# A hybrid encoder trunk on one core: where the up product's weight sums are made, and a seven-product down multiplication for the first token block

## The chip, the cores and the metric

The kernel runs on one core of one Trainium2 chip. The metric is the device time of one execution in microseconds. A core has TensorE (PE, matrix products, with its weight load shown apart as PEld), VectorE (DVE), ScalarE (ACT), GpSimd (POOL) and SyncE (SP), which here issues every DMA.

## What is computed

One layer of the trunk for 2048 prompt tokens and 32 sample tokens (2080 in all), model width 1024. A mixer (spatial gating and a gated delta rule) comes first; what the change alters is the feed-forward part behind it and its weights:

```python
    m, nb, ns, vr = mixer(h, conv_state[l], delta_state[l], w_in[l], ...)
    x = x + gt1 * m
    h = rmsnorm(x, norm_ffn_g[l]) * (1 + sc2) + sh2
    x = x + gt2 * (jnp.square(jax.nn.relu(h @ w_up[l])) @ w_down[l])
...
y = rmsnorm(x, final_norm_g)
```

`w_up` is 1024 x 4096 and `w_down` is 4096 x 1024, all float32.

## The kernel before

**Precision.** A float32 value is split into a high part, rounded to fp32r by ACT, and a low part, the difference, made by DVE (`split`, line 824; `operand`, line 1425). A product is three matmuls: high by high, high by low, low by high (`mm3`, line 411).

**Order of the work.** The whole program is written down as operations with an engine, a cost and the memory they touch (`Program.op`, line 218). `schedule` (line 237) then plays them through a model of the engines and puts them into one order. Where several are ready on an engine, a priority decides (`CHAIN, INV, LOCAL, EVAC, GEMM, IDLE`, line 55); from EVAC on, the place of the matmul that needs the result. On the chip each engine, SP too, runs its part of that order strictly from front to back, and waits where an operand or a buffer isn't there.

**The mixers** (`mixers`, line 856) take the first part of the time: input projections with weight slabs, the delta rule per head (`delta_local`, `delta_inv`, `delta_chain`), gating, and the output projection (`out_stage`, line 1331). `consts` (line 689) stands at their start. In `delta_chain` (line 1233) a chunk of 128 tokens goes PE, DVE, PE, ACT, PE, DVE, and the state `S` that the DVE writes last is what the next chunk's PE work reads.

**The feed-forward** (`feed_forward`, line 1509) goes over four token blocks of 520 tokens (two halves of 260). Per block there are 16 slabs of the hidden width (256 channels each). `ffn_up` (line 1572) multiplies a slab as 2x2 blocks by seven block products instead of eight (the Strassen-Winograd scheme): the token side's sums were made earlier (`h2_values`), the weight side needs four sums of the four weight blocks a11, a12, a21, a22. Two slabs form one step q of the down product. `ffn_down` (line 1674) does it by seven block products per half u of a step, `ffn_down8` (line 1715) by eight. Which one is taken is decided by `plain` (line 1506): for all steps of block 0, and for the last step of every block, the eight.

**Sums of the weights.** `up_weights(b, s)` (line 1430): in block 0 the four blocks are loaded, POOL makes the four sums (128x512 each), all seven operands are split (ACT and DVE), and the high and low parts of the four sums are written to memory (`su_d`, eight tiles of 128x512 a slab). Blocks 1 to 3 load three plain blocks, which are split, and the eight stored parts, which ACT alone rounds. `down_weights` (line 1469): block 0 loads and splits four plain blocks, and for even u makes the four sums on POOL and stores them (`sd_d`); in block 1 the sums of odd u are made the same way (`down_sums`, line 1484); otherwise they are loaded.

**Hidden values.** `hidden` (line 1626) splits the squared relu values into operands. With eight products there are four operands a slab; with seven there are seven for two slabs and each half-channel m, and four of them need a subtraction of 128x260, on POOL. Rings of buffers: `uraw` six buffers and `draw` four in block 0, joined to one ring of eight behind slab 15 of block 0; `rp8` for the hidden operands of block 0, `rpa` and `rpb` in the others.

Of the kernel before, what the change touches and what calls it, by code (L numbers as in the profile page):

```python
# [9 lines left out]
F32R = mybir.dt.float32r  # L10
AF = mybir.ActivationFunctionType
ALU = mybir.AluOpType
# [4 lines left out]
P = 128  # L17
# [101 lines left out]
class View:  # L119
# [55 lines left out]
    def pbc(self, n):  # L175
        return self.step("partition_broadcast", np.broadcast_to(np.uint8(0), (n,) + self.shape), self.reg, n)

# [145 lines left out]
class Kern:  # L323
# [211 lines left out]
    def setup(self):  # L535
# [74 lines left out]
        rg("va", [(q, 256 * e) for q in (18, 19, 20) for e in range(4)][:10], (P, 256))  # L610
        rg("raw", hv(18), (P, 516))
# [24 lines left out]
        self.su_d = [[[dt(f"su_d{s}_{i}{e}", [P, 512]) for e in range(2)] for i in range(4)] for s in range(16)]  # L636
# [52 lines left out]
    def consts(self):  # L689
# [3 lines left out]
        with self.p.at(GEMM):  # L693
# [19 lines left out]
            self.fill(self.z0, 0.0)  # L713

# [715 lines left out]
    def up_weights(self, b, s):  # L1430

        quad = lambda q: self.i["w_u"][s, q]
        if b == 0:
            a11, a12, a21, a22 = (self.raw(self.uraw, quad(q)) for q in range(4))
            s1, s2 = (self.turn(self.uraw) for _ in range(2))
            self.tt(s1, a21, a22, ALU.add, POOL)
            self.tt(s2, s1, a11, ALU.subtract, POOL)
        out = []

        def sum_(i, x):  # L1440
            if b == 0:
                hl = self.operand(self.uw, x)
                for e in range(2):
                    self.dma(self.su_d[s][i][e], hl[e].f32())
            else:
                hl = self.turn(self.uw)
                for e in range(2):
                    self.act(hl[e], self.raw(self.uraw, self.su_d[s][i][e]), AF.Copy)
            out.append(hl)

        plain = lambda q, x: out.append(self.operand(self.uw, x if b == 0 else self.raw(self.uraw, quad(q))))
        if b:
            s1 = s2 = s3 = s4 = a11 = a12 = a22 = None
        plain(0, a11)
        sum_(1, s2)
        sum_(0, s1)
        if b == 0:
            s3 = self.turn(self.uraw) if len(self.uraw) > 6 else a11
            self.tt(s3, a11, a21, ALU.subtract, POOL)
        sum_(2, s3)  # L1460
        if b == 0:
            s4 = s2
            self.tt(s4, a12, s2, ALU.subtract, POOL)
        sum_(3, s4)
        plain(1, a12)
        plain(3, a22)
        return out

# [377 lines left out]
```

## Time and profile before

| | us |
|---|---|
| runs shown: median (lowest to highest of 3) | 2415.27 (2406.06 to 2415.52) |
| the profiled execution's own time | 2432.54 |
| its span, first to last instruction | 2430.8 |
| mean granted TensorE clock | 0.996 |
| busy: PE, PEld, DVE, ACT, POOL | 2363.7, 2209.3, 1728.4, 1551.2, 757.9 |

The profiled execution is 17.3 us above the median of the runs. The stages in the trace: mixers from 0 to 1047 us, then the four token blocks, whose borders are at 1403, 1746 and 2084 us, and the end at 2431. Rows of groups read: line, engine, operation, written<-read tiles, shape, count, then busy time, mean ns of one, and the idle time before them with what ended it. Tile names: `f` is a PSUM bank of the feed-forward, `g`, `C`, `L`, `B`, `M` are PSUM banks of the mixers, `wh` and `wl` slab buffers for high and low parts, `BH` and `BL` the activations' high and low parts, `s` any of 25 SBUF slots, `wr` a raw weight buffer.

### The profile page before, as it was taken

The page shows a single profiled execution, that of the slowest core. Times are in us where ns is not written, and L with a number is a line of the kernel's source. Part 1 is how long each engine was busy: PE and PEld are TensorE (multiplying, and loading weights), DVE is VectorE, ACT ScalarE, POOL GpSimd, SP SyncE. Part 2 cuts the span into 40 slices and gives each one's busy share as a digit, 9 for nine tenths or more (in the row PEclk, how much of TensorE's full clock was granted, in tenths as well). Part 3 has the DMA queues.
Part 4 walks back from the last instruction along what each step waited for, and adds up shares of the span by engine and source line. Part 5 has one row for each costly group of instructions (what it writes and reads, how often), then busy time and mean ns, then how long its engine had stood idle before and what let it go on. Part 6 is the DMA issues. An engine that isn't in the chain of part 4 may idle for free.

```text
span 2430.8 us, 53532 instructions
## 1 busy us (share of the span) xinstructions
PE 2363.7 (97%) x18834; PEld 2209.3 (91%) x18834; DVE 1728.4 (71%) x3993; ACT 1551.2 (64%) x3705; POOL 757.9 (31%) x1055
## 2 busy tenths in 40 slices
PE   7999999999999999999999999999999999999998
PEld 4877778999989878999999999999999999999998
DVE  5556666556664646477777778889788878878796
ACT  4555556465655435365554688777897877877774
POOL 2134523212433223444434353323431212511111
PEclk9999999999999999999999999999999999999999
DMA  8688668455557767888766778786888878876773
GB/s 302 212 280 301 199 192 262 136 180 163 149 167 218 240 189 240 267 266 257 274 217 218 256 245 275 235 292 231 271 284 275 273 237 263 256 251 224 244 232 111
DMA packets 387238, 570.38 MB, mean 235 GB/s; under 512 B 71356, under 2 KB 201296, under 8 KB 386968
## 3 DMA queue, kind: packets, MB, share of 16 engines
q1 hardware_dynamic: 386968, 566.96, 72.5%
q8 instruction: 148, 2.42, 0.4%
q14 instruction: 122, 1.00, 0.1%
HBM read 432.44 MB, written 134.35 MB: 233 GB/s over the span
## 4 chain that ended last, share of the span: by engine, by line
PE 55%; DMA 17%; ACT 9%; DVE 9%; issue 5%; POOL 3%; SPq 1%; DVEq 0%; POOLq 0%; ACTq 0%
PE f L398 25%; PE g L398 22%; DVE s L352 5%; ACT s L337 5%; DMA s<-su_d 4%; PE C L398 3%; POOL s L352 2%; DMA s<-w_u 2%; ACT wh L337 2%; PE B L398 2%; DVE wl L352 1%; DVE s L357 1%; PE L L398 1%; SPq L390 1%; ACT wl L337 1%
## 5 line engine op out<-in xcount | busy, mean ns | idle before, releaser
L337 ACT ACTIVATE s<-s 128x260 fp32r<-128x260 f32 (+9 forms) x1379 | 601.6, 463 | 300.4 <-DVE s L357 82.0
L398 PE MATMUL f<-s,s 128*128 128x260 f32 x4068 | 541.3, 283 | 6.5 <-DVE s L352 4.9
L352 POOL TENSOR_TENSOR s<-s,s 128x260 f32<-128x260 f32 (+3 forms) x354 | 358.5, 1024 | 532.7 <-ACT s L337 400.1
L398 PE MATMUL f<-BH,wh 128*128 128x260 f32 x1796 | 511.1, 285 | 12.7 <-DVE s L352 11.1
L398 PEld LDWEIGHTS f<-s,s 128*128 128x128 f32 x4068 | 508.7, 188 | 11.0 <-DVE s L352 7.2
L398 PE MATMUL f<-BH,wl 128*128 128x260 f32 x1796 | 507.7, 283 | 1.1 <-DVE wl L352 1.1
L398 PE MATMUL f<-BL,wh 128*128 128x260 f32 x1796 | 506.4, 282 | 0.1
L352 DVE TENSOR_TENSOR s<-s,s 128x512 fp32r<-128x512 f32 (+5 forms) x721 | 412.3, 586 | 97.6 <-ACT s L337 63.4
L398 PE MATMUL g<-BH,wh 128*128 128x512 f32 (+2 forms) x1112 | 422.2, 380 | 0.0
L352 DVE TENSOR_TENSOR s<-f,s 128x260 f32<-128x260 f32 x856 | 345.0, 420 | 97.9 <-PE f L398 90.3
L398 PE MATMUL g<-BH,wl 128*128 128x512 f32 (+2 forms) x1112 | 392.9, 353 | 0.0
L398 PE MATMUL g<-BL,wh 128*128 128x512 f32 (+2 forms) x1112 | 391.6, 352 | 0.6 <-DVE BL L352 0.6
L398 PEld LDWEIGHTS f<-BH,wh 128*128 128x128 f32 x1796 | 337.7, 188 | 16.7 <-DVE s L352 8.2
L398 PEld LDWEIGHTS f<-BH,wl 128*128 128x128 f32 x1796 | 338.2, 188 | 1.9 <-DVE wl L352 1.9
L398 PEld LDWEIGHTS f<-BL,wh 128*128 128x128 f32 x1796 | 338.5, 188 | 0.3 <-DVE BL L352 0.3
L352 POOL TENSOR_TENSOR s<-s 128x260 f32<-128x260 f32 (+11 forms) x315 | 155.2, 493 | 475.7 <-DVE s L352 239.5
L337 ACT ACTIVATE wh<-s 128x512 fp32r<-128x512 f32 (+1 forms) x369 | 230.3, 630 | 78.6 <-DMA s<-w_u 28.3
L398 PEld LDWEIGHTS g<-BH,wh 128*128 128x128 f32 x1112 | 211.1, 190 | 26.6 <-issue 9.5
L398 PEld LDWEIGHTS g<-BH,wl 128*128 128x128 f32 x1112 | 210.2, 189 | 19.4
L398 PE MATMUL f<-BH,s 128*128 128x260 f32 x1016 | 225.5, 284 | 0.9 <-DVE s L352 0.8
L398 PEld LDWEIGHTS g<-BL,wh 128*128 128x128 f32 x1112 | 211.1, 190 | 15.0 <-DVE BL L352 1.1
L357 DVE SCALAR_TENSOR_TENSOR s<-s,s,s 128x512 f32<-128x512 f32 (+6 forms) x318 | 164.2, 533 | 76.0 <-ACT s L337 38.4
(119 smaller groups left out, 3537.7 us busy)
## 6 DMA issues: line engine op xcount, KB each, us to landing
s<-su_d SPq DMA_DIRECT2D x288, 256.0 KB, 3.9
s<-w_u SPq DMA_DIRECT2D x171, 256.0 KB, 4.2
s<-w_d SPq DMA_DIRECT2D x151, 256.0 KB, 4.2
s<-sd_d SPq DMA_DIRECT2D x106, 256.0 KB, 4.1
wr<-su_d SPq DMA_DIRECT2D x96, 256.0 KB, 4.4
wr<-w_b SPq DMA_DIRECT2D x42, 512.0 KB, 4.7
wr<-w_d SPq DMA_DIRECT2D x70, 256.0 KB, 4.8
s<-x_d SPq DMA_DIRECT2D x128, 130.0 KB, 3.9
```

The lines of the kernel that those rows point to most:

```text
L337: self.p.op(ACT, c, lambda: nc.scalar.activation(out=R(out), in_=R(in_), func=func, **{k: R(v) for k, v in kw.items()}), [out, accum], [in ...
L352: self.p.op(eng, c, lambda: e.tensor_tensor(out=R(out), in0=R(a), in1=R(b), op=op), [out], [a, b])
L357: self.p.op(DVE, c, lambda: nc.vector.scalar_tensor_tensor(out=R(out), in0=R(a), scalar=R(s), in1=R(b), op0=op0, op1=op1), [out], [a, s, b])
L390: self.p.op(DMA, max(500, x), lambda: nc.sync.dma_start(out=R(out), in_=R(in_)), [out], [in_], lat=DMA_LATENCY + min(0, x - 500))
L398: nc.tensor.matmul(R(out), R(l), R(r), **kw)
```

## The change

1. A method `up_sums` is called at the end of `consts`, with the lowest priority `IDLE`. It goes over the 16 slabs in four pieces of 128 columns each (64 pieces). A piece loads all four blocks by one DMA (128x4x128), makes the four sums in place on DVE (128x128 each), stores the four sums, and then twice rounds half of them on ACT (128x256) and stores the remainder that DVE forms (128x256). The first store holds the unrounded sums, the other two the low parts: the "two parts" in memory.
2. `up_weights` does in block 0 what blocks 1 to 3 did: three plain blocks loaded and split, eight stored parts loaded and rounded by ACT. POOL's sums and the eight stores a slab are gone from block 0.
3. `plain` is true for step 7 alone: block 0 does steps 0 to 6 by seven products. Its down sums are made in block 0 for all u below 14 (POOL, stored), and block 1 loads all of them.
4. The subtractions of the hidden values run on DVE in block 0, and on POOL in the others as before.
5. The rings are joined from the start, and `rp8` is gone.

```diff
@@ setup
+        rg("sh", [(8, 512), (9, 0), (10, 768), (14, 784)], (P, 2, 128))
+        rg("sx", [(4, 0), (4, 512)], (P, 4, 128))
...
-        self.su_d = [[[dt(f"su_d{s}_{i}{e}", [P, 512]) for e in range(2)] for i in range(4)] for s in range(16)]
+        self.su_d = [[dt(f"su_d{s}_{e}", [P, 4, 512]) for e in range(2)] for s in range(16)]
@@ consts
+        with self.p.at(IDLE):
+            self.up_sums()
+
+    def up_sums(self):
+
+        for n in range(64):
+            s, c = n // 4, slice(128 * (n % 4), 128 * (n % 4) + 128)
+            x = self.new("sx")
+            self.dma(x, self.i["w_u"][s, :, :, c].rearrange("q p c -> p q c"))
+            a11, a12, a21, a22 = (x[:, q] for q in range(4))
+            self.tt(a22, a21, a22, ALU.add)
+            self.tt(a21, a11, a21, ALU.subtract)
+            self.tt(a11, a22, a11, ALU.subtract)
+            self.tt(a12, a12, a11, ALU.subtract)
+            self.dma(self.su_d[s][0][:, :, c], x)
+            for h in (slice(2, 4), slice(0, 2)):
+                y = self.new("sh")
+                self.cp(y.f32r(), x[:, h], ACT)
+                self.tt(y, x[:, h], y, ALU.subtract)
+                self.dma(self.su_d[s][1][:, h, c], y)
@@ up_weights
+        for i, q in ((None, 0), (0, None), (3, None), (2, None), (1, None), (None, 1), (None, 3)):
+            if i is None:
+                out.append(self.operand(self.uw, self.raw(self.uraw, self.i["w_u"][s, q])))
+                continue
+            hl = self.turn(self.uw)
+            for e in range(2):
+                self.act(hl[e], self.raw(self.uraw, self.su_d[s][e][:, i]), AF.Copy)
             out.append(hl)
@@ down_sums
-        if b == 1 and u % 2:
+        if b == 0:
             a11, a12, a21, a22 = (get(quad(q)) for q in range(4))
-            s1, s2 = (self.turn(self.draw) for _ in range(2))
+            s1 = self.turn(self.draw)
...
-    def plain(self, b, q):
-        return b == 0 or q == 7
+    def plain(self, q):
+        return q == 7
@@ hidden
+        eng = POOL if b else DVE
         if s % 2 == 0 and g == 0:
             put("B11", t)
-            self.tt(k0, k1, t, ALU.subtract, POOL)
+            self.tt(k0, k1, t, ALU.subtract, eng)
```

Three places show how the order moves. **PE, the first down product of block 0.** Names: `f` PSUM banks, `s4` and `s5` the high and low part of a down weight, `s17`, `s18`, `s11`, `s19`, `s20`, `BH7`, `BL7` hidden operands. Before:

```order
L398 MATMUL f1_11807<-BH7_78,s4_1053 128x260
L398 MATMUL f1_11807<-BL7_86,s4_1053 128x260
L398 MATMUL f1_11807<-BH7_78,s5_10105 128x260
L398 MATMUL f1_11807<-s17_10865,s4_1053 128x260
L398 MATMUL f1_11807<-s18_11827,s4_1053 128x260
L398 MATMUL f1_11807<-s17_10865,s5_10105 128x260
L398 MATMUL f2_11894<-BH7_78,s4_1053 128x260
L398 MATMUL f2_11894<-BL7_86,s4_1053 128x260
```

and of the change:

```order
L401 MATMUL f1_12437<-s19_12364,s4_10858 128x260
L401 MATMUL f1_12437<-s20_12388,s4_10858 128x260
L401 MATMUL f1_12437<-s19_12364,s5_10752 128x260
L401 MATMUL f1_12437<-s11_11530,s4_10858 128x260 x2
L401 MATMUL f1_12437<-s11_11530,s5_10752 128x260
L401 MATMUL f2_12511<-s19_12364,s4_10858 128x260
L401 MATMUL f2_12511<-s20_12388,s4_10858 128x260
L401 MATMUL f2_12511<-s19_12364,s5_10752 128x260
```

The three matmuls of a product keep their form; what differs is how many products a step has (counted over the program, PE has 168 matmuls of this form fewer) and that some of the operands are now differences of hidden values.

**DVE, in the mixers, a chunk of the delta chain.** Names: `s13` is the chain's state and its right-hand side, `C` its PSUM banks, `s19` and `s18` gate values; in the change `s4` holds a piece's four blocks, and `s10` and `s14` its halves (among others). Before:

```order
L357 SCALAR_TENSOR_TENSOR s13_418<-C5_4516,s16_421,s1_406 128x128
L375 COPY s17_422<-g2_4357 128x4
L352 TENSOR_TENSOR s14_419<-s14_419,s17_422 128x2
L366 TENSOR_SCALAR s11_416<-s11_416,s14_419 128x128 x2
L352 TENSOR_TENSOR s14_419<-s17_422 128x1
L366 TENSOR_SCALAR s14_419<-s14_419 128x1
L357 SCALAR_TENSOR_TENSOR s12_417<-C4_4494,s17_422,s12_417 128x256
L357 SCALAR_TENSOR_TENSOR s19_424<-s19_424,s14_419,s16_421 128x256
L357 SCALAR_TENSOR_TENSOR s18_423<-s18_423,s14_419,s16_421 128x256
L375 COPY s17_422<-g0_4411 128x4
L357 SCALAR_TENSOR_TENSOR s13_418<-s13_418,s16_421,C5_4536 128x128
```

and of the change:

```order
L355 TENSOR_TENSOR s4_313<-s4_313 128x128
L369 TENSOR_SCALAR s14_323<-s14_323 128x1
L355 TENSOR_TENSOR s4_313<-s4_313 128x128 x2
L360 SCALAR_TENSOR_TENSOR s13_322<-C4_4722,s16_325,s1_310 128x128
L360 SCALAR_TENSOR_TENSOR s19_328<-s19_328,s14_323,s16_325 128x256
L360 SCALAR_TENSOR_TENSOR s18_327<-s18_327,s14_323,s16_325 128x256
L355 TENSOR_TENSOR s4_313<-s4_313 128x128
L355 TENSOR_TENSOR s10_319<-s4_313,s10_319 128x256
L355 TENSOR_TENSOR s14_323<-s4_313,s14_323 128x256
L360 SCALAR_TENSOR_TENSOR s13_322<-s13_322,s16_325,C4_4767 128x128
L355 TENSOR_TENSOR s11_320<-C4_4767,s13_322 128x128
```

Three operations of a piece now stand between the chain's right-hand side (`s13<-C4_4722`) and its state update (`s13<-s13,...,C4_4767`).

**SP, in the mixers.** Names: `pk_d`, `kq_d`, `us_d` are what the delta chain reads, `mix_d` what the mixers write, `s_d` and `z_d` gates. Before:

```order
L390 DMA s1_406<-us_d0_0_147 128x256
L390 DMA s1_406<-pk_d0_3_114 128x768
L390 DMA mix_d0_1_175<-s20_425 128x512
L390 DMA s20_425<-s_d_173 128x512
L390 DMA s8_413<-v_d2_103 128x256
```

and of the change:

```order
L393 DMA s1_310<-pk_d0_3_114 128x768
L393 DMA s20_329<-s_d_173 128x512
L393 DMA s19_328<-s_d_173 128x512
L393 DMA su_d4_1_222<-s8_317 128x2x128
L393 DMA su_d4_1_222<-s9_318 128x2x128
L393 DMA su_d4_0_221<-s4_313 512x1x128
L393 DMA su_d4_1_222<-s10_319 128x2x128
L393 DMA mix_d0_4_178<-s12_321 128x256
L393 DMA s12_321<-z_d0_105 128x256
```

Four stores of pieces stand between the mixers' own loads and stores. The 64 loads of pieces are spread over the mixers; the last store of a piece stands ahead of the first load of `su_d`.

82 lines of the change are left out of this document (21 added, 61 removed).

## The prediction

> **What bounds the kernel now.** I read the page first, then the table by stages, then what PE waits for in the stage that gets new work. The page's first part:
>
> ```profile
> PE 2363.7 (97%) x18834; PEld 2209.3 (91%) x18834; DVE 1728.4 (71%) x3993; ACT 1551.2 (64%) x3705; POOL 757.9 (31%) x1055
> ```
>
> PE is busy 97% of the span. That is an average, so the stages come next. The columns are the stretch, its length, and the busy time (and instructions) of PE, PEld, DVE, ACT and POOL, then clock, DMA share and GB/s; the first seven stretches are mixers, the last four the token blocks.
>
> ```profile
> core 0: us, PE busy (x) PEld busy (x) DVE busy (x) ACT busy (x) POOL busy (x), PEclk, DMA share, GB/s
> 0.00:130.00 130.00, 112.40 (x779) 80.97 (x780) 69.54 (x172) 61.83 (x118) 25.12 (x34) 1.00 0.77 255
> 130.00:300.00 170.00, 168.12 (x783) 126.77 (x782) 104.80 (x226) 99.42 (x237) 76.54 (x121) 1.00 0.80 265
> 300.00:450.00 150.00, 147.62 (x1518) 126.62 (x1516) 97.38 (x296) 86.42 (x256) 40.66 (x98) 1.00 0.68 209
> 450.00:600.00 150.00, 148.85 (x1231) 143.96 (x1230) 91.58 (x294) 86.56 (x227) 29.36 (x89) 1.00 0.55 166
> 600.00:750.00 150.00, 145.51 (x1326) 136.67 (x1324) 91.20 (x274) 89.55 (x257) 49.62 (x138) 0.98 0.53 159
> 750.00:900.00 150.00, 147.80 (x1257) 125.92 (x1257) 84.61 (x248) 66.65 (x192) 42.40 (x84) 0.99 0.73 225
> 900.00:1047.00 147.00, 143.94 (x846) 133.25 (x845) 83.82 (x180) 63.25 (x142) 53.32 (x52) 0.99 0.79 244
> 1047.00:1403.00 356.00, 347.54 (x2869) 344.65 (x2870) 269.82 (x492) 205.05 (x467) 150.14 (x119) 1.00 0.75 249
> 1403.00:1746.00 343.00, 334.20 (x2736) 329.07 (x2735) 291.38 (x602) 270.11 (x617) 129.57 (x131) 1.00 0.81 262
> 1746.00:2084.00 338.00, 332.01 (x2731) 328.08 (x2730) 275.79 (x601) 271.14 (x627) 88.73 (x106) 1.00 0.81 262
> 2084.00:2431.00 347.00, 335.70 (x2777) 333.32 (x2775) 268.46 (x614) 251.17 (x572) 72.41 (x88) 0.99 0.67 217
> ```
>
> PE is the bound in every stage after the first 130 us. Behind 130 us the mixers leave it 15.2 us idle of 917 (917 less 901.84), and PE's waits in that part are small and scattered:
>
> ```profile
> PE B L398 <- issue: 3.7, 1, 3.7
> PE M L398 <- POOL s L352: 2.6, 1, 2.6
> PE C L409 <- DVE s L366: 1.6, 1, 1.6
> PE C L398 <- DVE s L357: 1.0, 3, 0.7
> ```
>
> Blocks 0 to 2 show what a block costs with eight and with seven products. Block 0 (all eight) takes 356 us, block 1 (seven, POOL still making half of the down sums) 343, block 2 (seven, all sums loaded) 338. What one feed-forward matmul takes of PE's time is seen best where nothing disturbs it, the last step of block 0. The columns are start, length, engine, line, operation:
>
> ```profile
> 1382.07 21.80 PE L398 MATMUL f<-s,s 128*128 128x260 f32 x180
> 1403.71 0.28 PE L398 MATMUL f<-BH,wh 128*128 128x260 f32 x1
> ```
>
> (1403.71 - 1382.07) / 180 = 0.1202 us, start to start; 0.28 is the latency of one. With it the rest of each block, stalls and small work, is 356 - 2869 x 0.1202 = 11.1 us in block 0, 343 - 2736 x 0.1202 = 14.1 in block 1, 338 - 2731 x 0.1202 = 9.7 in block 2.
>
> **Term 1, the products.** A step by eight products is 192 matmuls, by seven 168; seven steps of block 0 change, so 7 x 24 = 168 fall away, 168 x 0.1202 = 20.2 us. PE sets the end there, so all of it counts as long as the other engines keep up.
>
> **Term 2, the rest of block 0.** Block 0 becomes a block 1 with one addition: its hidden subtractions are on DVE. These are 56 (8 a step, 7 steps).
>
> ```profile
> L352 DVE TENSOR_TENSOR s<-s,s 128x260 f32<-128x260 f32 x16 | 7.0, 454 | 0.5 <-DMA s<-x_d 0.5
> L352 DVE TENSOR_TENSOR s<-s,s 128x512 fp32r<-128x512 f32 x80 | 66.5, 839 | 6.6 <-ACT s L337 6.4
> L352 DVE TENSOR_TENSOR s<-s,s 128x512 fp32r<-128x512 f32 x80 | 57.6, 726 | 3.5 <-ACT s L337 3.4
> ```
>
> The first row is such an operation in block 1: 56 x 0.454 = 25.4 us. DVE would then have 291.4 + 25.4 = 317 us of work. The other two rows are the weight splits of block 1 and block 2, the same operation at 839 and 726 ns; POOL was busy 129.6 and 88.7 us there, so a busier POOL goes with a slower DVE. POOL in block 0 loses 64 sums of the up weights and gains 28 of the down weights:
>
> ```profile
> L352 POOL TENSOR_TENSOR s<-s,s 128x512 f32<-128x512 f32 x47 | 67.9, 1446 | 26.1 <-DVE wl L352 22.6 <-ACT wh L337 1.4
> ```
>
> At 1.446 us each that is 150.1 - 36 x 1.446 = 98 us, between blocks 1 and 2. So I take 5 to 12 us off DVE and put it at 305 to 312 us in a block of about 343: 90%, where block 1 has 85% with 14.1 us of rest and block 2 82% with 9.7. Extrapolating that rise (4.4 us for 3 points of load) gives 20 to 22; I take 18, since the subtractions come back in 0.45 us where POOL took 0.86. Bounds: 10 (as block 2) and 39, if DVE's own 312 plus as much idle time as it has today in block 1 (343 - 291.4 = 51.6) set the length: 363.6 us. So block 0 comes to 2701 x 0.1202 + 18 = 342.7, which is 13.3 less than 356. POOL's sums in front of the first up product go too, and its operands come straight from memory; I count no gain for that.
>
> The Trainium skill, page "SBUF — State Buffer", section "Who interferes with whom", says that a DVE instruction with two SBUF inputs and a GpSimd instruction that reads SBUF exclude each other for a whole instruction. The 839 against 726 ns agree in direction. Without such exclusion DVE would stay at 317 us and term 2 at the higher end, some 4 us worse; by the rule it is as taken above. In the mixers the same rule speaks against the change, as 384 new operations of DVE, nearly all with two SBUF inputs, meet POOL's work.
>
> **Term 3, block 1.** It loses 28 POOL sums and their stores, and loads sums instead, as block 2 does: 343 towards 338. I take 4 us off (bounds 0 and 5). Blocks 2 and 3 keep their work: 0, give or take 2.
>
> **Term 4, the mixers.** Here the 64 pieces are new. Per piece: DVE four operations of 128x128 and two of 128x256, ACT two of 128x256, SP four DMAs. No row shows the sums themselves; the nearest are
>
> ```profile
> L352 DVE TENSOR_TENSOR s<-C,s 128x128 f32<-128x128 f32 x64 | 18.1, 284 | 0.0
> L352 DVE TENSOR_TENSOR BL<-s,BH 128x256 fp32r<-128x256 f32 x16 | 7.6, 479 | 1.3 <-ACT BH L337 1.1
> L337 ACT ACTIVATE s<-s 128x256 f32<-128x256 f32 x59 | 24.6, 421 | 20.7 <-DVE s L357 13.5 <-issue 5.6 <-ACT wh L337 0.7
> L390 SPq DMA_DIRECT2D s<-kq_d x72: 523/530/1214, 192.3 to 915.0; - x72
> q1 hardware_dynamic: 386968, 566.96, 72.5%
> ```
>
> DVE: 256 x 0.284 + 128 x 0.479 = 134 us, onto 623 of 1047 (the seven rows summed), 72% instead of 60. ACT: 128 x 0.421 = 54, onto 554, 58%. SP: 256 issues at the median 0.53 (the row of a DMA with many rows to describe) = 136 us. DMA: 64 x 768 KB = 50.3 MB; 566.96 MB took 72.5% of 2430.8 us, 3.1 us a MB, so 156 us, onto 726 (each of the seven shares times its stretch): 84% of 1047. Each engine has room; lowest priority puts the pieces into gaps. So the cover is the idle time of DVE, ACT and DMA beside a PE that never stops. What is not hidden is order: each queue runs front to back. Behind a sum that waits for its load, DVE holds the chain's state update; behind a store that waits for DVE, SP holds the loads of the delta chain and of the weight slabs; and a load into one of the two piece buffers waits until the store from it has landed. Rows for what such a wait costs:
>
> ```profile
> DVE s L357 <- DMA s<-gc_d: 10.4, 4, 8.0
> POOL s L352 <- DMA s<-w_u: 77.8, 8, 12.4
> SPq L390 <- DMA x_d<-s: 17.4, 15, 4.5
> ```
>
> DVE on a load: 2.6 us a time; SP on a landing: 1.2 a time. POOL's 9.7 is an engine with nothing else to do. If each piece held DVE for 0.5 us, and PE felt a quarter of it (it has projection matmuls between the chain's), that is 64 x 0.125 = 8 us. I take 9 us for the mixers. Bounds: 0 (a little below if the new order of PE falls better), and 64 x 2.6 / 4 = 42 us.
>
> **The sum.** -20.2 + (18 - 11.1) - 4 + 9 = -8.3 us. From the profiled execution's 2432.5 that is 2424.2; the median of the runs shown lies 17.3 lower, so from 2415.3 I forecast 2407. A measurement of this kernel tells about 0.5%, 12 us, from no change.
>
> **Rivals.**
>
> A. The mixers hide the pieces, and block 0 runs as block 2: -20.2 - 1.4 - 5 = -27 at the best (9.7 instead of 11.1 us of rest, block 1 at its bound), -17 with terms 2 and 3 as forecast. For it: PE's waits in the mixers behind 130 us are 15 us in 917, although DVE is as often late there as anywhere. Against: one engine in order always passes something on. 2389 to 2398.
>
> B. Slower: the pieces hold the in-order queues in the mixers. Place: the first sum of a piece on DVE, and its stores on SP. Price: with 0.6 us passed on to PE per piece, 38 us, less 17.3 gained behind, 2436; it turns the result to slower by over 12 us from (17.3 + 12) / 64 = 0.46 us a piece. For it: lowest-priority work is placed right where its load is expected, without slack, and DMA's share is already 0.77 to 0.80 in three of the seven stretches. Against: the rows above show DVE hardly ever waiting on a load today.
>
> C. DVE becomes the bound of block 0: 363.6 us instead of 342.7. Then -20.2 + (39 - 11.1) - 4 + 9 = +13 at the worst, +2 halfway (28.5 us of rest): 2417 to 2428. For it: 90% by the sum. Against: block 1 runs with 85% and PE's stalls there are 14 us in all.
>
> D. The change does not bring what it says: PE's 168 matmuls are gone by the order, so this can only be a loss of the same size elsewhere, which B and C hold. It has no chance of its own.
>
> **Chances.** Forecast (2400 to 2414) 0.40, A 0.25, B 0.22, C 0.13. For eight in ten the range takes in A but for its last part, the forecast, C, and B up to its price: 2390 to 2436. Faster by over 0.5% (under 2403): most of A and a third of the forecast, 0.36. Slower by over 0.5% (above 2427): nearly all of B and a quarter of C, 0.25. The rest, 0.39, is within.
>
> **What would show it.** In the table by stages of the changed kernel: block 0 at 343 us with about 2700 PE instructions, DVE 305 to 312 in it and POOL about 98; block 1 at 339; blocks 2 and 3 within 2 us; the mixers' end 9 us later than 1047. B shows as PE idle time behind DVE and ACT in the mixers, with DVE rows of the pieces waiting for `w_u` and SP waiting on landings. C shows as PE's waits for DVE in block 0 growing past 20 us. A shows as mixers that end at 1047 again. The forecast is wrong if the mixers' end moves by over 20 us or block 0 doesn't fall under 350.

## The result, and the profile after

The changed kernel takes 2451.13 us (median of 5 runs, 2444.36 to 2452.36) where the kernel before takes 2415.27 (2406.06 to 2416.77): 36 us slower, a ratio of 1.0145 with a 95% interval of 1.0124 to 1.0166. The forecast was 2407 in a range of 2390 to 2436; the time is above its upper end. The profiled execution took 2452.03 us, its span is 2450.2.

The page's first part, as shown of before:

```profile
PE 2359.4 (96%) x18666; PEld 2192.6 (89%) x18666; DVE 1838.2 (75%) x4537; ACT 1651.9 (67%) x3980; POOL 677.0 (28%) x991
```

PE has its 168 matmuls fewer (18666 against 18834) and is busy 4.3 us less, but the span is 19.4 us longer than the profiled span of before. The table by stages has the columns of the one before; the last four rows are the token blocks, cut where the first up matmul of a block starts.

```profile
core 0: us, PE busy (x) PEld busy (x) DVE busy (x) ACT busy (x) POOL busy (x), PEclk, DMA share, GB/s
0.00:130.00 130.00, 109.70 (x764) 78.10 (x765) 77.50 (x203) 65.01 (x129) 24.57 (x33) 1.00 0.88 287
130.00:300.00 170.00, 165.90 (x772) 124.69 (x771) 116.03 (x277) 104.21 (x248) 75.85 (x120) 0.99 0.92 299
300.00:450.00 150.00, 145.93 (x1392) 123.28 (x1392) 111.88 (x355) 92.68 (x274) 44.08 (x89) 1.00 0.87 264
450.00:600.00 150.00, 146.56 (x1303) 139.25 (x1304) 114.19 (x397) 92.61 (x250) 33.30 (x88) 1.00 0.88 263
600.00:750.00 150.00, 146.81 (x1341) 137.78 (x1340) 115.73 (x374) 97.35 (x293) 54.34 (x146) 1.00 0.78 232
750.00:900.00 150.00, 146.52 (x1275) 126.25 (x1273) 92.01 (x284) 73.66 (x208) 45.46 (x84) 1.00 0.85 256
900.00:1052.00 152.00, 151.81 (x895) 139.97 (x893) 79.96 (x181) 63.69 (x143) 47.75 (x47) 1.00 0.74 230
1052.00:1409.00 357.00, 336.50 (x2712) 328.98 (x2712) 314.15 (x658) 270.39 (x622) 104.98 (x88) 1.00 0.81 263
1409.00:1757.00 348.00, 336.71 (x2726) 329.96 (x2725) 274.38 (x603) 270.42 (x620) 87.64 (x105) 1.00 0.79 255
1757.00:2097.00 340.00, 334.00 (x2733) 330.50 (x2732) 274.60 (x602) 270.93 (x626) 88.00 (x106) 0.99 0.80 261
2097.00:2450.00 353.00, 338.94 (x2778) 333.83 (x2776) 267.73 (x612) 250.91 (x571) 71.04 (x88) 0.99 0.65 213
```

The mixers end at 1052, 5 us later than before, with 18.5 us of PE idle behind 130 us (922 less the six rows' 903.5) where it was 15.2. PE's largest waits between 130 and 1040 us are still small:

```profile
PE L L401 <- ACT s L340: 4.3, 6, 1.3
PE C L401 <- DVE s L360: 3.3, 5, 1.2
PE B L401 <- DMA s<-adaw: 2.2, 1, 2.2
```

The work of each stage is what was forecast: 2712 PE instructions in block 0 (about 2700), DVE 314 us there (305 to 312), POOL 105 (98). The length is not. Block 0 takes 357 us where 343 was forecast, and **blocks 2 and 3, whose instructions the change does not touch, are 2 and 6 us longer than in the first profile of before**. Blocks 0, 1 and 3 have PE idle that their own work does not explain: with 0.1202 us a matmul the rest is 357 - 2712 x 0.1202 = 31.0 us in block 0, 348 - 2726 x 0.1202 = 20.3 in block 1, which has less work than block 1 of before with its 14.1, and 353 - 2778 x 0.1202 = 19.1 in block 3 (before 347 - 2777 x 0.1202 = 13.2). The pace itself did not change; one row after another in the last steps of block 0 of the changed kernel:

```profile
1380.83 0.28 PE L401 MATMUL f<-BH,wl 128*128 128x260 f32 x1
1380.95 0.28 PE L401 MATMUL f<-BH,wh 128*128 128x260 f32 x1
1381.07 0.28 PE L401 MATMUL f<-BL,wh 128*128 128x260 f32 x1
1381.19 0.28 PE L401 MATMUL f<-BH,wl 128*128 128x260 f32 x1
```

That is 0.12 us from start to start, so the time is lost between matmuls, in waits. PE's own waits name DVE and ACT (below), and one step further back, what ACT waits for in the four blocks (1050 to 2400 us; total, times, longest) begins with

```profile
ACT wh L340 <- DMA s<-su_d: 53.9, 55, 2.2
ACT s L340 <- PE f L401: 38.4, 55, 1.9
ACT wl L340 <- DMA s<-su_d: 36.5, 45, 2.0
```

ACT waits longest for the loads of the stored sums. The change altered one thing about them that my forecast did not look at: each of the eight parts of a slab was an array of its own, `[P, 512]`, whose 128 rows of 2 KB follow one another. Now four parts share one array `[P, 4, 512]`: the 128 rows of one load still are 2 KB each, but begin 8192 bytes apart.

**The theories tested.** P (place): that distance of 8 KB makes the loads of the sums land later, in all four blocks. C (continuity, not the forecast's rival of that letter): rows that don't follow one another are slower, whatever the distance. Rival B of the forecast: the pieces hold the queues in the mixers. H, rival C of the forecast: DVE bounds block 0 by its hidden subtractions. The first expectations use other letters: there M is the forecast's rival B, L is P, and B is the theory that the loss arises in block 0 by the seven products or by DVE (H).

### The profile page after: what moved, and what is told of

Read it like the earlier page. It is cut to its first block, busy times and chain, and to the rows that moved or that the text cites. A ratio compares the mean times of both kernels' runs of the same rounds, so it can differ in the third digit from the quotient of the medians.

```text
span 2450.2 us, 54456 instructions
## 1 busy us (share of the span) xinstructions
PE 2359.4 (96%) x18666; PEld 2192.6 (89%) x18666; DVE 1838.2 (75%) x4537; ACT 1651.9 (67%) x3980; POOL 677.0 (28%) x991
## 2 busy tenths in 40 slices
DMA packets 490366, 622.10 MB, mean 254 GB/s; under 512 B 75532, under 2 KB 303776, under 8 KB 490088
## 4 chain that ended last, share of the span: by engine, by line
PE 30%; DMA 16%; DVE 13%; ACT 9%; issue 5%; POOL 1%; SPq 0%; DVEq 0%; ACTq 0%; POOLq 0%
PE f L401 16%; PE g L401 11%; DVE s L355 9%; DMA s<-su_d 6%; ACT s L340 5%; ACT wh L340 2%; DMA wr<-su_d 2%; DMA s<-w_u 2%; PE C L401 2%; DVE s L360 1%; ACT wl L340 1%; DVE wl L355 1%; DVE BL L355 1%; DMA s<-th_d 1%; DMA s<-w_d 1%
## 5 line engine op out<-in xcount | busy, mean ns | idle before, releaser
L340 ACT ACTIVATE s<-s 128x260 f32<-128x260 f32 (+11 forms) x1576 | 678.7, 462 | 264.9 <-DVE s L355 105.3
L355 DVE TENSOR_TENSOR s<-s,s 128x512 fp32r<-128x512 f32 (+6 forms) x960 | 511.0, 547 | 100.3 <-ACT s L340 72.5
L401 PE MATMUL f<-BH,wh 128*128 128x260 f32 x1796 | 513.6, 286 | 17.3 <-DVE s L355 13.9
L401 PEld LDWEIGHTS f<-s,s 128*128 128x128 f32 x3900 | 495.6, 189 | 25.0 <-DVE s L355 15.2
L355 POOL TENSOR_TENSOR s<-s,s 128x260 f32<-128x260 f32 (+3 forms) x309 | 291.1, 954 | 530.6 <-ACT s L340 415.6
L355 DVE TENSOR_TENSOR s<-f,s 128x260 f32<-128x260 f32 x928 | 369.5, 417 | 80.4 <-PE f L401 77.7
L340 ACT ACTIVATE wh<-s 128x512 fp32r<-128x512 f32 (+1 forms) x352 | 219.2, 630 | 85.1 <-DMA s<-su_d 53.9
L401 PE MATMUL f<-BH,s 128*128 128x260 f32 x1016 | 236.4, 285 | 5.2 <-ACT BH L340 4.4
```

The lines of the kernel that those rows point to most:

```text
L340: self.p.op(ACT, c, lambda: nc.scalar.activation(out=R(out), in_=R(in_), func=func, **{k: R(v) for k, v in kw.items()}), [out, accum], [in ...
L355: self.p.op(eng, c, lambda: e.tensor_tensor(out=R(out), in0=R(a), in1=R(b), op=op), [out], [a, b])
L401: nc.tensor.matmul(R(out), R(l), R(r), **kw)
```

## The experiments

The kernel before had medians of 2415.3 to 2423.1 us from one set of runs to another, so runs are compared by their ratio to the before of the same set (95% interval behind). 0.001 is 2.4 us. The stages of the profiled executions, cut at the first up matmul of each block:

| kernel | mixers | block 0 | block 1 | block 2 | block 3 | ratio to before |
|---|---|---|---|---|---|---|
| before | 1046.8 | 356.9 | 342.6 | 338.1 | 346.4 | 1 |
| before_again | 1048.7 | 354.1 | 338.2 | 333.8 | 347.2 | 1 |
| after | 1052.1 | 356.5 | 348.8 | 340.0 | 352.8 | 1.0145 (1.0124 to 1.0166) |
| sums_only | 1051.6 | 353.5 | 353.3 | 345.6 | 358.3 | 1.0157 (1.0127 to 1.0187) |
| hidden_pool | 1048.5 | 355.5 | 343.2 | 348.5 | 357.5 | 1.0147 (1.0104 to 1.0190) |
| layout | 1060.4 | 345.0 | 334.2 | 333.8 | 344.9 | 0.9972 (0.9954 to 0.9989) |
| before_pitch | 1047.8 | 359.3 | 349.2 | 340.8 | 355.9 | 1.0127 (1.0100 to 1.0155) |
| pad, 9 KB | 1055.2 | 346.7 | 336.3 | 334.1 | 346.5 | 0.9990 (0.9971 to 1.0008) |
| gap, 2.25 KB | 1052.3 | 348.8 | 339.4 | 335.4 | 345.2 | 0.9976 (0.9960 to 0.9993) |
| layout_pool | 1057.8 | 343.2 | 335.0 | 333.3 | 344.1 | 0.9988 (0.9969 to 1.0007) |
| pitch4k | 1054.3 | 346.7 | 338.2 | 335.9 | 350.8 | 1.0033 (1.0010 to 1.0055) |
| pitch12k | 1053.5 | 346.7 | 335.7 | 339.3 | 345.9 | 0.9990 (0.9972 to 1.0008) |
| pitch16k | 1050.3 | 350.4 | 336.8 | 338.4 | 350.1 | 1.0029 (1.0010 to 1.0047) |
| move_only | 1062.8 | 342.7 | 333.1 | 333.7 | 347.5 | 0.9982 (0.9963 to 1.0002) |
| halves | 1043.9 | 344.6 | 334.1 | 332.0 | 346.2 | 0.9935 (0.9914 to 0.9956) |
| halves_pad | 1047.5 | 346.3 | 335.5 | 333.8 | 346.0 | 0.9951 (0.9932 to 0.9970) |
| before_halves | 1036.2 | 353.9 | 337.8 | 332.1 | 344.9 | 0.9963 (0.9947 to 0.9980) |

A stage comes from one execution; between the two profiles of the same kernel before the blocks differ by up to 4.4 us, so a difference of that size in one row says nothing by itself. The granted clock has a part in this. The traces have a few stretches of 3.4 us, some of 6.8, in which the clock is 0.50; in one of them (hidden_pool, 1124.0 to 1127.4 us) the matmuls of the feed-forward start 0.217 us apart instead of 0.12, so 3.4 us of it cost an estimated 1.5 us. The mixers have 13.7 us of them in before and layout, 17.1 in before_again and move_only, 6.8 in before_halves, 3.4 in the changed kernel and halves_pad and none in hidden_pool and halves.

**before_again**: the kernel before, for a second profile. No edit.

> The kernel before, unchanged, for a second profile: its first profiled execution lay 17 us above its median, so the stage borders of that one may not be typical. M (the pieces cost time in the mixers, some 20 to 30 us): a typical execution near 2415 us ends its mixers near 1030 us instead of 1047. B (block 0 lost its gain and the later blocks became slower): the mixers end near 1047 again and the token blocks are shorter than 357, 343, 338 and 346 us.

2423.71 us in one run, 2420.91 the median of before in this set. The mixers end at 1048.7, so the 1030 that M asks for is not borne out. The first profile's block 1 and block 2 were 4 us longer than this one's: the 17.3 us by which that profile lay above its median sat partly there, spread over the stages and not in the end alone.

**sums_only**: the sums' pieces in the mixers and the stored parts stay; the down product of block 0 is by eight again.

```diff
-    def plain(self, q):
-        return q == 7
+    def plain(self, b, q):
+        return b == 0 or q == 7
```

> One part alone: the pieces in the mixers and their use in block 0, but block 0's down product by eight block products with half of the down sums, as before. M: the loss is in the mixers, so this is as slow as the changed kernel or slower, 2445 to 2465 us. B: the seven products in block 0 are what costs; this stays near the kernel before, 2410 to 2425 us, with block 0 at 350 to 356.

1.0157: the loss is there without the seven products, so it belongs to the sums. The time of 2463.32 us lies in M's range, but not by M's mechanism: the mixers end at 1051.6, 3 to 5 us later than before, and the rest of the loss stands in blocks 1 to 3. Block 0 shows no loss here, though its loads of the sums are as new: by eight products DVE and ACT have more idle time than in the changed kernel,

```profile
1052.00:1405.00 353.00, 348.40 (x2873) 345.53 (x2873) 212.00 (x433) 233.50 (x538) 63.64 (x61) 1.00 0.76 247
```

212 us of 353 for DVE where the changed kernel has 314 of 357, and a rest of 353 - 2873 x 0.1202 = 7.7 us. So loads placed the same way show no cost where the engines behind them have room (this trace doesn't tell when they landed). Its blocks 2 and 3 are 5 us longer than the changed kernel's with the same work; why is open.

**hidden_pool**: the hidden subtractions of block 0 back on POOL.

```diff
-        eng = POOL if b else DVE
+        eng = POOL
```

> The changed kernel with the 56 subtractions of hidden values in block 0 on POOL instead of DVE. B (DVE at 88% in block 0 sets its length): DVE loses 25 us there, PE's rest in block 0 falls from 31 us towards 20, the time from 2451 to about 2440. M or L: 2448 to 2455.

1.0147, as the changed kernel, so the move gains nothing in all. Block 0 alone can't decide it:

```profile
1048.50:1404.00 355.50, 338.56 (x2708) 331.66 (x2708) 301.34 (x601) 270.72 (x624) 154.93 (x144) 0.98 0.82 265
```

DVE has 13 us less work there, not 25, POOL 50 us more, and the granted clock of the stage is 0.98 where the changed kernel had 1.00, which may hide a gain of some 5 us (an estimate: 13.7 us at half clock against 3.4). What rules H out is the next run: there DVE works 313 us in block 0, as in the changed kernel, and the block takes 345 us.

**layout**: each sum's half by itself; the order of every engine's instructions stays that of the changed kernel, only addresses differ.

```diff
-        self.su_d = [[dt(f"su_d{s}_{e}", [P, 4, 512]) for e in range(2)] for s in range(16)]
+        self.su_d = [[dt(f"su_d{s}_{e}", [4, P, 512]) for e in range(2)] for s in range(16)]
...
-            self.dma(self.su_d[s][0][:, :, c], x)
+            self.dma(self.su_d[s][0][:, :, c].re("q p c -> p q c"), x)
```

> The changed kernel with each stored sum as one piece of memory (4 x 128 x 512) instead of rows of 512 elements 2048 apart, so that loads of a sum read 256 KB in one run. L (the loads of the sums became slower by their place in memory, and block 1 to 3 with them): blocks 1 and 3 come back to 343 and 346 us, the time falls by 10 to 15 us to about 2438. M or B: within 4 us of 2451.

0.9972: the whole loss is gone, and a little more, where 10 to 15 us of gain were expected. Against the changed kernel's 1.0145 this is 0.0173, or 42 us, for addresses alone. The DMA packets are the same in number and size as well (490366 packets, 622.10 MB, 303776 of them under 2 KB, in both). Blocks 0 to 3 of this kernel:

```profile
1060.00:1405.00 345.00, 332.47 (x2707) 326.48 (x2706) 312.73 (x658) 270.11 (x622) 106.32 (x88) 1.00 0.84 273
1405.00:1740.00 335.00, 331.65 (x2739) 328.85 (x2738) 276.67 (x605) 269.52 (x620) 88.58 (x106) 1.00 0.83 265
1740.00:2073.00 333.00, 329.77 (x2725) 327.66 (x2725) 275.34 (x602) 271.18 (x626) 88.67 (x104) 1.00 0.83 266
2073.00:2418.00 345.00, 335.40 (x2777) 332.96 (x2775) 267.45 (x612) 250.76 (x571) 70.75 (x88) 0.99 0.68 218
```

DVE's and ACT's busy time is that of the changed kernel within 3 us a stage, PE's is 4 to 5 us less and its idle time shrinks further; the blocks are 12, 13, 7 and 8 us shorter. DMA's share for what it moves is the same (0.81 at 263 GB/s in block 0 of the changed kernel, 0.84 at 273 here), so the packets themselves don't take longer in the changed kernel. What ACT waits for in the four blocks of layout:

```profile
ACT wh L340 <- DMA s<-su_d: 26.8, 34, 2.1
ACT wl L340 <- DMA s<-su_d: 20.9, 37, 2.0
```

48 us where the changed kernel has 90. The issue rows of block 0 (count, KB each, median us from issue to landing) of the changed kernel:

```profile
s<-su_d SPq DMA_DIRECT2D x102, 256.0 KB, 4.8
```

and in layout:

```profile
s<-su_d SPq DMA_DIRECT2D x102, 256.0 KB, 4.1
```

These two medians rest on few loads: the trace has the landing of 12 of the 102 in either kernel. The surer figures are the waits, and the landings of the next run. DVE's largest wait in that block is 21.6 us in the changed kernel and 12.3 in layout:

```profile
DVE s L355 <- ACT s L340: 21.6, 24, 3.3
```

```profile
DVE s L355 <- ACT s L340: 12.3, 18, 2.2
```

PE's waits in that block of the changed kernel:

```profile
PE f L401 <- DVE s L355: 12.8, 15, 2.2
PE f L401 <- ACT BH L340: 4.4, 3, 2.7
```

and in layout:

```profile
PE f L401 <- DVE s L355: 7.0, 11, 1.7
PE f L401 <- ACT BH L340: 2.8, 2, 1.7
```

This is the path of the loss: the load later (by 0.7 us in these medians), ACT late with the rounding, DVE late behind ACT, PE idle. The wait that PE shows names an engine that was only passing it on.

**before_pitch**: the kernel before, with its sums placed as in the changed kernel and nothing else.

```diff
-        self.su_d = [[[dt(f"su_d{s}_{i}{e}", [P, 512]) for e in range(2)] for i in range(4)] for s in range(16)]
+        self.su_d = [[dt(f"su_d{s}_{e}", [P, 4, 512]) for e in range(2)] for s in range(16)]
```

> The kernel before with one thing changed: the stored sums lie as in the changed kernel (128 x 4 x 512, so that the 128 rows of 2 KB of one load are 8 KB apart). The order on every engine stays. P (8 KB from row to row makes the loads of the sums late) and C (a load reads faster when its bytes lie in one run) both give 20 to 30 us more, 2435 to 2448, all of it in blocks 1 to 3, as block 0 only writes them. If the rows' place has no part in it, and what the layout run gained came from the writes, this stays within 5 us of the kernel before.

1.0127, 31 us slower than before, a little more than the 20 to 30 expected, without any work in the mixers and without the seven products. Blocks 1 to 3 are 19 us longer together than in the first profile of before and 27 longer than in before_again; block 0, which only writes the sums, is 2 to 5 us longer. The loads between 1400 and 2400 us in before:

```profile
s<-su_d SPq DMA_DIRECT2D x276, 256.0 KB, 4.0
```

and in before_pitch:

```profile
s<-su_d SPq DMA_DIRECT2D x278, 256.0 KB, 4.3
```

The medians rest on 108 and 109 landings, and before_again has 4.0 too. ACT's waits for `s<-su_d` in the four blocks are 59 us, against 43 and 38 in the two profiles of before. Before loads 384 of these parts (blocks 1 to 3), the change 512 (block 0 too). 31 us / 384 is 0.080 us a load, 42 us / 512 is 0.082. That the two averages agree is partly chance, and they are no price of a single load: sums_only loads 512 and its block 0 shows no loss. With layout this shows from both sides that the place of the rows costs the time, and the forecast's rival B falls as the cause of the loss. Whether the distance or the broken run does it, the next two runs decide.

**pad** and **gap** separate the distance from continuity. pad keeps the changed kernel's array and adds 1 KB to each row of it; gap keeps layout's order and puts 256 bytes between its rows.

```diff
+        self.su_d = [[dt(f"su_d{s}_{e}", [P, 4, 576]) for e in range(2)] for s in range(16)]
```

```diff
+        self.su_d = [[dt(f"su_d{s}_{e}", [4, P, 576]) for e in range(2)] for s in range(16)]
```

> The changed kernel with 64 unused elements behind each 512 of a stored sum, so that the rows of a load lie 9 KB apart instead of 8 KB; everything else is the same, and a load is still not one run. P (the power of two from row to row): the time comes back to 2410 to 2422. C (one run or not): it stays at 2445 to 2455.

> The layout run with 64 unused elements behind each row of 512: rows of 2 KB with 256 bytes between them, no longer one run of 256 KB. P: as the layout run, 2410 to 2420. C: slow as the changed kernel, 2440 to 2455.

0.9990 and 0.9976: rows 9216 or 2304 bytes apart cost nothing that can be told from rows that follow one another. C falls. ACT's waits in pad:

```profile
ACT wh L340 <- DMA s<-su_d: 30.1, 37, 2.3
ACT wl L340 <- DMA s<-su_d: 22.8, 36, 1.4
```

**layout_pool**: layout, and a piece's four sums on POOL instead of DVE.

```diff
-            self.tt(a22, a21, a22, ALU.add)
+            self.tt(a22, a21, a22, ALU.add, POOL)
```

(and the other three alike)

> The layout run with the four sums of each piece on POOL instead of DVE; the order of the mixers moves with it. M (sums that wait for their load hold DVE, and with it the delta chain): the mixers, which ended at 1060 us in the layout run, end 5 to 10 us earlier, and the time is 2405 to 2410. Rival: the pieces' cost in the mixers is that of their DMAs and of SP, then the mixers stay within 3 us of 1060 and the time at 2412 to 2420.

0.9988, not better than layout's 0.9972 within the intervals. The mixers end at 1057.8, within 3 us of layout's as the rival said: DVE without the four sums a piece doesn't make them shorter.

**pitch4k, pitch12k, pitch16k**: which distances delay. pitch4k is layout with `[4, P, 1024]`, the other two are the changed kernel with `[P, 4, 768]` and `[P, 4, 1024]`; only the first 512 values of a row are used.

> The layout run's kernel, with each row of a sum's half given 4 KB of memory instead of 2 (2 KB data, 2 KB unused), so that the 128 rows of one load begin 4096 bytes apart. If every power of two above the row's own length delays the load as 8 KB does: 2440 to 2455 us, loads of the sums landing at a median of 4.2 to 4.4 us in blocks 1 to 3. If only 8 KB and more do: 2410 to 2422, landing at 3.8 to 4.0.

> The changed kernel with the rows of one load 16384 bytes apart instead of 8192. If the delay comes from a large power of two as the distance: 2445 to 2465 us, loads of the sums landing at 4.2 us or later. If 8 KB alone is special (rows that fall on the same place as those of the neighbouring array, say): 2412 to 2422.

> The changed kernel with the rows of one load 12288 bytes apart. If only powers of two delay a load: as the pad run, 2412 to 2422 us, landing at 3.8 to 4.0 us in blocks 1 to 3. If any multiple of 4 KB does: 2425 to 2445, landing at 4.1 or later, as in pitch4k and pitch16k.

12 KB is as good as 9 KB (0.9990), 4 KB and 16 KB are slightly worse than no change (1.0033 and 1.0029), and 8 KB is far worse (1.0145). For 4 and 16 KB the times fell between what either theory expected: some delay, some 10 us against 9 and 12 KB, a quarter of that of 8 KB. The landings don't settle it: in blocks 1 to 3 the median is 4.1 us for 4 KB and 3.9 for 16 KB, where 4.2 and more were expected, against 4.3 in the changed kernel and 3.9 in layout and pad, each from some 35 loads; the trace of pitch12k has none. ACT's waits of pitch4k stand between those of layout and the changed kernel as well:

```profile
ACT wh L340 <- DMA s<-su_d: 37.9, 50, 1.9
ACT wl L340 <- DMA s<-su_d: 25.8, 35, 2.3
```

So of the distances tried 4, 8 and 16 KB are the bad ones and 2.25, 9 and 12 KB are not: powers of two above the row's own length, as far as these go (in layout the rows of 2 KB begin 2 KB apart, and that costs nothing). That a multiple of 4 KB as such does no harm rests on 12 KB alone. Why 8 KB is the worst of the three is not settled.

**move_only**: layout, where a piece is only loaded and stored; it leaves out the four additions, the rounding and the remainders, so the stored parts are not sums.

```diff
-            self.tt(a22, a21, a22, ALU.add)
...
-                self.cp(y.f32r(), x[:, h], ACT)
-                self.tt(y, x[:, h], y, ALU.subtract)
-                self.dma(self.su_d[s][1][h, :, c].re("q p c -> p q c"), y)
+                self.dma(self.su_d[s][1][h, :, c].re("q p c -> p q c"), x[:, h])
```

> The layout run's kernel, in which the pieces are only loaded and stored: it leaves out the four additions, the rounding and the remainders of the sums, so what block 0 and later blocks read as sums are plain blocks of the weights. It keeps the transfers and SP's issues of the pieces. If the transfers and issues cost the mixers their 5.6 us: the mixers end as in the other runs with pieces, 1053 to 1055 us, and the time stays at 2412 to 2420. If DVE's and ACT's work on the pieces costs it: the mixers end near 1048, and the time is 2405 to 2411.

The mixers end at 1062.8, no earlier than layout's 1060.4, and the time is the same. The table by stages from 130 us to the end of the mixers, in layout:

```profile
130.00:1060.00 930.00, 907.25 (x6977) 795.63 (x6976) 629.21 (x1864) 525.99 (x1420) 298.95 (x574) 0.99 0.84 256
```

in move_only:

```profile
130.00:1063.00 933.00, 907.42 (x6970) 796.15 (x6968) 541.71 (x1517) 493.97 (x1304) 286.25 (x574) 0.99 0.83 255
```

and in before_again, without pieces:

```profile
130.00:1049.00 919.00, 901.92 (x6945) 794.30 (x6944) 552.32 (x1515) 491.71 (x1306) 287.99 (x579) 0.99 0.68 211
```

DVE falls from 629 to 542 us and ACT from 526 to 494, and the stage does not shorten. What is left of the pieces is their transfers: DMA's share is 0.83 against 0.68. So what the pieces cost the mixers doesn't come with the arithmetic. It comes with the transfers, their issues, or the changed order of the engines around them; which of these was not tried.

**halves, before_halves, halves_pad**: the inputs that the mixers load by half slabs have rows of 4 KB that begin 8192 bytes apart, the same distance (those of `w_v`, 8 of the loads, have 4160 bytes and begin 8320 apart). These three keep each half by itself: halves is layout, halves_pad is pad, and before_halves the kernel before, each with

```diff
-            self.dma(raw, src[:, s])
+            self.dma(raw, src[e])
...
-            self.dma(w, self.i["ada0"][f, :, 1024 * e : 1024 * e + 1024])
+            self.dma(w, self.i["ada0"][f, e])
...
-                self.dma(w, self.i["adaw"][j - 1, k, :, 1024 * e : 1024 * e + 1024])
+                self.dma(w, self.i["adaw"][j - 1, k, e])
...
+    for n in ("ada0", "adaw", "w_v", "w_b", "w_o"):
+        t = a[n]
+        t = t.reshape(t.shape[:-1] + (2, t.shape[-1] // 2))
+        a[n] = np.moveaxis(t, -2, -3)
```

> The layout run's kernel, and the inputs that the mixers load by half slabs (w_b, w_v, w_o, ada0, adaw: rows of 4 KB that begin 8192 bytes apart) are kept with each half by itself, so that the rows of a load follow one another. If the distance of 8 KB delays these loads too and the mixers wait for them: the mixers end 5 to 15 us earlier than the layout run's, 2398 to 2410 us in all. If PE doesn't wait for them: within 4 us of the layout run's kernel, 2410 to 2419.

> The kernel before, with the half slabs of w_b, w_v, w_o, ada0 and adaw each kept by itself, as in the halves run. If these loads' distance of 8 KB costs the mixers time in any case: 8 to 14 us below the kernel before, ratio 0.994 to 0.997, mixers ending 8 to 14 us earlier. If it does so only beside the pieces' transfers: within 4 us of the kernel before.

> The halves run's kernel, with the sums kept as in the pad run (rows of one load 9216 bytes apart, stores as in the changed kernel). If the mixers pay for stores into rows that follow one another (1060 and 1063 us in layout and move_only against 1052 and 1055 in after and pad): the mixers end 3 to 8 us earlier than in halves and the time is 2398 to 2403 us. If those were the spread from one execution to the next: 2404 to 2410.

before_halves is at 0.9963, halves at 0.9935, halves_pad at 0.9951. Each is 0.0037 to 0.0039 below the kernel that it was made from (before 1, layout 0.9972, pad 0.9990). The kernel before itself paid some 9 us for the place of its half slabs: its mixers end at 1036.2 instead of 1047 to 1049, of which an estimated 3 to 5 us are the clock. PE's weight load waits less for one of these loads; up to 1040 us, in before and in before_halves:

```profile
PEld B L398 <- DMA s<-adaw: 10.0, 12, 2.6
PEld B L398 <- DMA s<-adaw: 4.3, 5, 1.3
```

and in layout and in halves:

```profile
PEld B L401 <- DMA s<-adaw: 10.2, 11, 1.7
PEld B L401 <- DMA s<-adaw: 6.3, 8, 2.0
```

The landings of these loads decide nothing, as the traces have too few of them (in layout and halves 8 of 42 for `w_b` and 4 of 32 for `adaw`). The ratios carry the verdict. The three runs put each half into one run of memory, so for these rows the distance of 8 KB was not told apart from rows that don't follow one another. halves is the fastest kernel of the study, 0.65% below before (2405.99 us where before took 2423.09 in the same set). halves_pad is not faster than halves, and its mixers end later (1047.5 against 1043.9, with 3.4 us more at half clock): that stores into rows that follow one another cost the mixers time, as layout's 1060.4 suggested, is not borne out.

What the change itself is worth where nothing lies 8 KB apart is halves against before_halves: 0.9935 / 0.9963 = 0.9972, with the two intervals' half widths (0.0021 and 0.0017) combined as 0.0027, so 0.9945 to 0.9999, or 7 us faster, give or take 7 (8 was forecast). layout against before gives the same 0.9972.

## Why the prediction was wrong

The failed step is one sentence of term 3, "Blocks 2 and 3 keep their work: 0, give or take 2", and with it the sentence of term 2 on block 0's up product, "its operands come straight from memory; I count no gain for that". Both take a load of a sum to be the same load as before, because it has the same size. The diff showed that it was not (`[P, 512]` became `[P, 4, 512]`); I read it as bookkeeping and gave it no term. It costs 42 us (layout against the changed kernel, 31 in the kernel before), which is all but 2 of the 44 us between forecast and result. By the forecast's own sign, block 0 had to fall under 350 us; it took 356.5. What is left of the change without that distance is 7 us, give or take 7, where the sum had 8; the stages of the single executions below add up to 1 to 5, so the near agreement is in part luck.

The other terms, each against kernels with a better distance, as means of the profiled executions of layout, pad, gap, pitch12k, halves and halves_pad beside those of before, before_again and before_halves:

| term | forecast | measured |
|---|---|---|
| 1 and 2, block 0: 20.2 off, 6.9 back | -13.3 | 355.0 to 346.4: -8.6 |
| 3, block 1 | -4 | 339.5 to 335.9: -3.6 |
| 3, blocks 2 and 3, well placed | 0 | 334.7 to 334.7, 346.2 to 345.8: -0.4 |
| 4, mixers | +9 | +7.7 and +11.3 (halves and halves_pad against before_halves) |
| place of the sums | none | +42 |

**Term 1** was right: 168 matmuls fewer at an unchanged 0.12 us.

**Term 2** was near in size: layout's block 0 has a rest of 345 - 2707 x 0.1202 = 19.6 us, 18 was forecast. The row of the hidden subtractions (with a few other operations of that shape) in block 0 of the changed kernel and one of POOL's sums there:

```profile
L355 DVE TENSOR_TENSOR s<-s,s 128x260 f32<-128x260 f32 x50 | 24.0, 500 | 0.6 <-ACT s L340 0.5
L355 POOL TENSOR_TENSOR s<-s 128x512 f32<-128x512 f32 x14 | 19.8, 1413 | 46.1 <-DVE s L355 41.2 <-ACT wh L340 2.1 <-ACT s L340 1.9
```

500 ns where I took 454, 1413 where I took 1446. DVE's work in block 0 came to 313 to 314 us, so of the 5 to 12 us that a less busy POOL was to take off the 317 only 3 to 4 came off. The gain of -8.6 instead of -13.3 has to do with its base as well: the first profile of before, from which I worked, had a block 0 of 356.9, the other two 354.1 and 353.9.

**Term 4** had about the right size for a reason that the runs don't bear out. The forecast let DVE, held behind a load, pass a quarter of a wait on to PE. The rows of the pieces in the mixers of the changed kernel are

```profile
L355 DVE TENSOR_TENSOR s<-s 128x128 f32<-128x128 f32 x256 | 73.1, 297 | 20.5 <-DMA s<-w_u 18.3
L340 ACT ACTIVATE s<-s 128x256 fp32r<-128x256 f32 x128 | 51.5, 417 | 37.6 <-DVE s L355 36.9
```

so the durations (0.284 and 0.421 forecast) and the waits for the load (18.3 / 64 = 0.29 us a piece, 0.5 assumed) were about right, but move_only has none of these instructions and its mixers are as long. What is left is the transfers, their issues and the order around them; how these reach PE was not tried further. Against the two plain profiles of before, term 4 looks smaller and scattered: the mixers of the kernels with whole pieces, and with the half slabs as in before, end anywhere from 1048.5 to 1060.4. Much of the scatter is the clock. With an estimated 0.45 us taken off for each us at half clock, both profiles of before end their mixers at 1041, these kernels at 1048 to 1054 and move_only at 1055, so the pieces cost 8 to 13 us in each of them, and halves and halves_pad 11 and 13 against before_halves.

**Rival B** had the price nearest to the result, 2436, and the wrong place: the mixers end 5 us later, some 10 at equal clock, not 38. That a number comes closest says nothing of the mechanism; the table by stages does. **Rival C** gave 2417 to 2428; its sign, waits of PE for DVE in block 0 past 20 us, did not show (14.3 us in the changed kernel), and layout's block 0 is short with the same work on DVE. **Rival A** fell by the mixers, which end later in every kernel with pieces at equal clock, and by layout's block 0, whose rest is 19.6 us and not 9.7.

The Trainium skill, page "DMA: Bandwidth & Descriptors", section "Latency and other measured facts", has a row on row pitches in HBM of large powers of two: copies with a pitch of 512 KiB and more lose bandwidth, and a few KiB of padding bring it back. Here a loss shows at a pitch far below those it lists, 8 KB (a landing of 4.3 us instead of 4.0 in before_pitch, 1.0127), and 1 KB of padding suffices (1.0145 to 0.9990). No run here shows what in the memory or the DMA engines makes it so; the page calls its own mechanism an inference, too.

## What to carry to other kernels

When a change packs several arrays into one, write down for each load how long a run is and how far apart the runs begin; a power of two above the length of a run, 8 KB above all, can be a cost even where size, count and order of the loads stay the same, and a few hundred values of padding or a separate array each take it away. In a forecast give every array whose shape changes a term of its own, and look at the stages whose work does not change: when they get longer, the cause is shared, and not in the step that was meant to change. Then look for the same distance in what was there before; here the kernel before gained 0.4% from it.

## What was not expected of the hardware

- A load of 128 rows of 2 KB takes longer from issue to landing when the rows begin 8192 bytes apart: a median of 4.3 us against 4.0 in before_pitch and before, and 31 and 42 us of two kernels' time. 9216 and 12288 bytes are within the intervals as good as rows that follow one another (0.9990 twice, against 0.9972), 4096 and 16384 lie between (1.0033, 1.0029). The share of the DMA engines' time for what they move stays the same; what else delays the landing is open.
- Rows of 4 KB that begin 8192 bytes apart cost time as well: with each half by itself the kernel before is at 0.9963, and its mixers end 11 to 13 us earlier, an estimated 8 at equal clock. Here the distance was not separated from the broken run.
- In the mixers, some 88 us more of DVE work and 32 of ACT work (the rows of layout and move_only above) cost PE nothing that can be seen: move_only, without it, ends its mixers no earlier (1062.8 against 1060.4).
- A stretch of 3.4 us with a granted clock of 0.50 (matmuls 0.217 us apart instead of 0.12) moves the end of a stage by an estimated 1.5 us. Four or five of them in the mixers of one execution and none in those of another make 6 to 8 us, as much as the effect that was looked for there.
